# Low halves of weights made early, and lists, taps and fetches moved, in a two-block transformer kernel

## The chip, the cores and the metric

The kernel runs on one core of one Trainium2 chip, in a single launch. The metric is the device time of one execution in microseconds (us); the figure before is the median of three runs. Engine names are those of the profile: PE is the matrix engine, PEld its weight load, DVE the vector engine, ACT the scalar engine, POOL the GpSimd engine, SP the engine that only issues transfers.

## The reference

Two blocks follow each other on one sequence of 512 tokens, 1024 wide, all in float32.

- First block: an RMS norm, one input projection, a sliding-window attention (8 query heads, 2 key heads, blocks of 128) beside a convolution of width 31 over 512 channels with a layer norm and a pointwise product; their concatenation goes through `w_out`, is normed and added. Then a gated feed-forward layer (1024 to 2816 to 1024), normed and added.
- Second block: a norm and one projection; a gated spatial unit; an attention that keeps the 128 best keys of a scored list; two sigmoid gates and an output product. Then `peer`: queries of 8 heads x 2 halves are scored against 128 keys each, the 16 best of each half are combined into 16 experts of 16384 for each head, and the output is the sum over these 128 experts of gate x gelu(x . u_e) x v_e:

```
sub = einsum('bshpd,hpnd->bshpn', q, subkeys)
s_top, i_top = top_k(sub, 16)
best, pos = top_k(s_top[0] + s_top[1], 16)
a = gelu(einsum('td,ted->te', x, u_tab[expert]))
y = einsum('te,ted->td', softmax(best) * a, v_tab[expert])
```

## The kernel before, in words

Tokens lie in four blocks `tb` of 128. A weight comes in units of 128 x 1024 (`unit`, lines 132 to 142): SP's queue loads `raw`, ACT casts it to a rounded high half `whi` (line 138), and DVE subtracts for the low half `wlo` (line 140). Each product is then three matmuls, high x high, high x low and low x high (`mm3`, lines 155 to 158). The rings `raw`, `whi` and `wlo` have four buffers each.

The program is written as one list of calls, and a scheduler orders each engine's instructions from that list; side work (convolution taps, attention, top-k lists) is written as generators, which `advance` draws on beside the projections by a written estimate in us (`CONV_US`, `ATT_US`, `TOPK_US`, `TOP_US`, `R_US`).

- Convolution and first attention (lines 324 to 548). Each channel group has 31 taps; of groups 2 and 3 the first 12 and 8 run on PE as diagonal matmuls (`pe_taps`, line 363), the others on DVE (line 368). `att1(b)` makes scores (435, 439), softmax (446 to 460), transposes (466) and the value product (469). A bias table comes back from DRAM as `rev` (403) and is flipped on PE (405), all four parts ahead of the queries.
- `transition` (248 to 304) ends a layer: sums of squares, `rsqrt` (160 to 165: a DVE instruction, then a power on POOL, line 164), scaling, transposes (183).
- Feed-forward layer (559 to 575): 44 units, 24 matmuls of 512 columns each.
- Second block: index scores (`index_block`), top-k on DVE (`topk`, 709 and 710), queries, then for each `tb` the key and value product into a PSUM bank `kv` (744 to 747), norm and rotation (750 to 758), `turn` (735). The table `wsT` is masked by four POOL instructions (816).
- `peer`. The 16 query units give `sub`; `top_keys` (968 to 977) makes a list for each of 64 (block, half-head) pairs; `keys` (979) combines and builds experts' numbers through one-hots (1030, 1031) and matmuls (1034, 1036); `build` (1091) spreads gates into a table `g_dram`. Beside that PE runs 100 of the 128 blocks of `peer_u` for 320 tokens (`u_block`, 930), the results going to `a_dram`. Tokens past 320 are done by gathered rows (`gathered`, 946): 192 gathers of `peer_u` rows and 128 of `peer_v`, each followed by one DVE instruction (949, 957, 964).
- Last stage (1199 to 1260). For each pair of blocks `second` (1218) multiplies the stored activations `al` by the gates `gl` (line 1228), splits the product into `wvhi` and `wvlo`, and `v_block` runs 18 matmuls of 512 columns for each of 128 blocks of `peer_v`. `al` (line 1211) and `gl` (line 1225) are fetched where they are first used.

```
with order(after[0]):
    lead[0] = S.copy(hi[:, :n], raw[:, :n]).ins
with order(after[1]):
    pace[0] = V.tensor_tensor(lo[:, :n], raw[:, :n], hi[:, :n].bitcast(F32), op=OP.subtract).ins
```

## Time and profile before

| what | value |
|---|---|
| median of three runs | 2129.66 us (2129.12 to 2134.75) |
| the profiled execution | 2132.12 us |
| its span, first to last instruction | 2130.4 us |
| PE busy | 2061.1 us (97%) |
| DVE busy | 1573.1 us (74%) |
| ACT busy | 825.7 us (39%) |
| POOL busy | 520.2 us (24%) |
| mean granted PE clock | 0.988 |
| bytes moved, mean rate | 476.47 MB, 224 GB/s |

A busy PE is one that has a matmul under way; its ends are modelled, so what tells of lost time are the pauses, the engine that ended each, the granted clock, and the number of matmuls in a stretch. Stages with their own limits follow each other: attention and convolution until about 250 us, the feed-forward layer until 590, the second block until 960, `peer`'s queries until 1047, lists and blocks of `peer_u` until 1484, and the products with `peer_v` from there.

### The profile page before, as it was taken

How to read it: one execution, taken by the hardware profiler on the slowest of the kernel's cores; microseconds unless marked ns; L12 is line 12 of the kernel's file. 1: busy time of each engine (PE TensorE's matmuls, PEld its weight loads, DVE VectorE, ACT ScalarE, POOL GpSimd, SP SyncE). 2: the span in 40 equal slices, each digit the busy share in tenths (PEclk: the TensorE clock that was granted, in tenths of full speed). 3: DMA queues.
4: the chain of work that ended last, by engine and by line, in shares of the span. 5: the costliest groups of instructions: out<-in, count | busy, mean ns of one | idle time of the engine just before them, and what ended most of it. 6: DMA issues, size and time to landing. Idle time of an engine off the chain costs nothing.

```text
span 2130.4 us, 29554 instructions
## 1 busy us (share of the span) xinstructions
PE 2061.1 (97%) x11128; PEld 1753.5 (82%) x11128; DVE 1573.1 (74%) x2901; ACT 825.7 (39%) x1339; POOL 520.2 (24%) x383
## 2 busy tenths in 40 slices
PE   7989999999989999999999999999999999999999
PEld 6746888888877877888889899999888878788887
DVE  6974633332268955455699999998999988899997
ACT  5354422221244342333453455555433333333332
POOL 1000000000010000000032222220575656566573
PEclk9998999999999999999999999999999999999999
DMA  5202232333222222333278889899999999999995
GB/s 188 82 28 69 72 107 93 95 99 117 84 87 80 70 89 69 109 124 98 81 288 278 289 299 358 290 365 307 390 394 411 389 402 387 410 402 411 411 399 223
DMA packets 163281, 476.47 MB, mean 224 GB/s; under 512 B 13865, under 2 KB 57265, under 8 KB 161218
## 3 DMA queue, kind: packets, MB, share of 16 engines
q1 hardware_dynamic: 67104, 259.70, 34.2%
q0 software_dynamic: 46656, 169.18, 20.9%
q10 hardware_dynamic: 49378, 45.71, 6.5%
q8 instruction: 87, 1.43, 0.3%
q14 instruction: 56, 0.46, 0.1%
HBM read 432.18 MB, written 42.09 MB: 223 GB/s over the span
## 4 chain that ended last, share of the span: by engine, by line
PE 54%; DVE 21%; issue 13%; DMA 8%; POOL 3%; ACT 2%; DVEq 0%; POOLq 0%; SPq 0%; ACTq 0%
PE bank_a L156 12%; PE bank_a L157 12%; PE bank_a L158 12%; DVE wlo L140 5%; PE bank_b L156 4%; PE bank_b L157 4%; PE bank_b L158 4%; DMA rows<-in_peer_u_dram,gidx 2%; DVE rows L957 2%; POOL rows L941 2%; DMA rows<-in_peer_v_dram,gidx 2%; DMA al<-a_dram 2%; DVE h L964 2%; DVE rows L949 2%; PE bank_b L1108 1%
## 5 line engine op out<-in xcount | busy, mean ns | idle before, releaser
L138 ACT CAST whi<-raw 128x1024 fp32r<-128x1024 f32 (+1 forms) x413 | 431.9, 1047 | 884.0 <-PE bank_a L157 332.0
L140 DVE TENSOR_TENSOR wlo<-raw,whi 128x1024 fp32r<-128x1024 f32 (+1 forms) x413 | 499.9, 1213 | 265.9 <-ACT whi L138 263.6
L156 PE MATMUL bank_a<-xhi,whi 128*128 128x320 f32 (+2 forms) x1600 | 549.3, 344 | 0.8 <-ACT xhi L152 0.8
L158 PE MATMUL bank_a<-xhi,wlo 128*128 128x320 f32 (+2 forms) x1600 | 546.2, 342 | 3.3 <-DVE wlo L140 3.3
L157 PE MATMUL bank_a<-xlo,whi 128*128 128x320 f32 (+2 forms) x1600 | 548.0, 343 | 0.6 <-DVE xlo L153 0.6
L941 POOL DMA_INDIRECT rows<-in_peer_u_dram,gidx x192 | 279.0, 1453 | 553.4 <-DVE gidx L1042 143.1
L158 PEld LDWEIGHTS bank_a<-xhi,wlo 128*128 128x128 f32 x1600 | 303.5, 190 | 31.6 <-DVE wlo L140 5.3
L156 PEld LDWEIGHTS bank_a<-xhi,whi 128*128 128x128 f32 x1600 | 302.8, 190 | 28.3 <-ACT xhi L152 1.8
L157 PEld LDWEIGHTS bank_a<-xlo,whi 128*128 128x128 f32 x1600 | 303.7, 190 | 26.9 <-DVE xlo L153 1.6
L941 POOL DMA_INDIRECT rows<-in_peer_v_dram,gidx x128 | 206.2, 1611 | 115.2 <-DVE h L964 91.2
L164 POOL TENSOR_TENSOR rstd<-rstd,neghalf 128x1 f32<-128x1 f32 (+2 forms) x37 | 25.2, 682 | 844.2 <-DVE rstd L163 832.4
L156 PE MATMUL bank_a<-whi,wvhi 128*128 128x512 f32 x512 | 201.9, 394 | 7.4 <-ACT wvhi L152 7.3
L157 PE MATMUL bank_a<-wlo,wvhi 128*128 128x512 f32 x512 | 202.0, 394 | 1.7 <-DVE wlo L140 1.6
L158 PE MATMUL bank_a<-whi,wvlo 128*128 128x512 f32 x512 | 201.7, 394 | 1.7 <-DVE wvlo L153 1.6
L964 DVE SCALAR_TENSOR_TENSOR h<-rows,ga,h 128x1024 f32<-128x1024 f32 x128 | 164.1, 1282 | 5.6 <-DMA rows<-in_peer_v_dram,gidx 4.2
L957 DVE SCALAR_TENSOR_TENSOR rows<-rows,h 128x1024 f32<-128x1024 f32 x128 | 152.8, 1220 | 9.9 <-DMA rows<-in_peer_u_dram,gidx 9.9
L156 PEld LDWEIGHTS bank_a<-whi,wvhi 128*128 128x128 f32 x512 | 97.0, 189 | 28.7 <-ACT wvhi L152 9.1
L158 PEld LDWEIGHTS bank_a<-whi,wvlo 128*128 128x128 f32 x512 | 97.2, 190 | 24.9 <-DVE wvlo L153 4.2
L157 PEld LDWEIGHTS bank_a<-wlo,wvhi 128*128 128x128 f32 x512 | 97.0, 189 | 21.6 <-DVE wlo L140 2.4
L156 PE MATMUL bank_b<-whi,wvhi 128*128 128x512 f32 x256 | 99.9, 390 | 0.0
L158 PE MATMUL bank_b<-whi,wvlo 128*128 128x512 f32 x256 | 99.6, 389 | 0.0
L157 PE MATMUL bank_b<-wlo,wvhi 128*128 128x512 f32 x256 | 99.6, 389 | 0.0
(403 smaller groups left out, 3272.5 us busy)
## 6 DMA issues: line engine op xcount, KB each, us to landing
raw<-in_wt_dram SPq DMA_DIRECT2D x150, 512.0 KB, 3.6
raw<-in_ut_dram SPq DMA_DIRECT2D x128, 512.0 KB, 5.8
raw<-in_peer_v_dram SPq DMA_DIRECT2D x128, 512.0 KB, 8.0
g_dram<-gt ACTq DMA_DIRECT2D x24, 896.0 KB, 7.9
gl<-g_dram SPq DMA_DIRECT2D x14, 1536.0 KB, 10.6
a_dram<-ab ACTq DMA_DIRECT2D x25, 640.0 KB, 5.6
al<-a_dram SPq DMA_DIRECT2D x25, 640.0 KB, 9.3
rows<-in_peer_u_dram,gidx POOLq DMA_INDIRECT x192, 9.1
```

Of the source, the lines that this page charges most:

```text
L138: lead[0] = S.copy(hi[:, :n], raw[:, :n]).ins
L140: pace[0] = V.tensor_tensor(lo[:, :n], raw[:, :n], hi[:, :n].bitcast(F32), op=OP.subtract).ins
L156: T.matmul(o, lh, rh, start=start, stop=False)
L157: T.matmul(o, lh, rl, start=False, stop=False)
L158: T.matmul(o, ll, rh, start=False, stop=stop)
L164: G.tensor_tensor(r, r, neghalf[:, :shape[1]], op=OP.pow)
L941: G.indirect_dma_start(out=r, out_offset=None, in_=table, in_offset=bass.IndirectOffsetOnAxis(ap=idx[:, k:k + 1], axis=0))
L949: V.scalar_tensor_tensor(r, r, 1.0, hn2, op0=OP.mult, op1=OP.mult, accum_out=ga2[:, k:k + 1])
L957: V.scalar_tensor_tensor(r, r, 1.0, hn3, op0=OP.mult, op1=OP.mult, accum_out=ga[:, k:k + 1])
L964: V.scalar_tensor_tensor(h[3], r, ga[:, k:k + 1], h[3], op0=OP.mult, op1=OP.add)
L1108: T.matmul(gp[:, j, :], o_[:, g2, :, t2], oh1[:, g2, :, t2], start=o_ is ohs[0], stop=o_ is ohs[-1])
```

## The change

Low halves are made ahead: in the feed-forward loop `make_low` runs twice for each of the 22 columns. It loads one of 44 units through POOL's queue, casts it on ACT, subtracts on DVE and stores the low half to DRAM through POOL's queue. The 44 are the 16 units of the queries and the first 28 blocks of `peer_u`. Where a unit has such a low half, `unit` fetches it into `wlo` through ACT's queue in place of the subtraction.

The lists of blocks 0 and 1 are drawn on beside the queries too, behind those of blocks 2 and 3; the written estimates there grow by `LOW_US`. `al` is fetched one step ahead with three buffers, `gl` a group ahead in three pieces. The 12 PE taps of group 2 become 8, and the PE taps are issued inside the attention of blocks 2 and 3 while their DVE taps join at once; the four parts of the bias are spread over the queries; the first products with `w_out` move behind the mean of the layer norm; the four key and value products move beside the query units, evacuated by ACT; the masks of `wsT` are put behind a power; two square sums are added inside the instruction that adds the epsilon.

```diff
-N_PE_TAPS = (0, 0, 12, 8)
+LOW_US = 1.0
+N_PE_TAPS = (0, 0, 8, 8)
-SA_BUFS = 4
+SA_BUFS = 7
+N_EARLY = 28
...
-    def unit(src, n=1024, after=(None, None)):
+    def unit(src, n=1024, after=(None, None), low=None):
...
+        if low is not None:
+            nc.scalar.dma_start(lo[:, :n].bitcast(F32), low[:, :n])
         with order(after[0]):
             lead[0] = S.copy(hi[:, :n], raw[:, :n]).ins
+        if low is not None:
+            return hi, lo
...
+    early = [(wt[p], lows, p) for p in range(wt.shape[0] - 16, wt.shape[0])] + \
+            [(A["ut"][i], ulows, i) for i in [2 * p + j for p in SPAIR for j in range(2)][:N_EARLY]]
+
+    def make_low(wk):
+        if not early:
+            return
+        src, where, key = early.pop(0)
+        raw = wk.tile([128, 1024], F32, name="eraw", bufs=2)
+        nc.gpsimd.dma_start(raw, src)
+        lo = wk.tile([128, 1024], F32R, name="elow", bufs=2)
+        with order(lead[0]):
+            S.copy(lo, raw)
+        with order(pace[0]):
+            V.tensor_tensor(lo, raw, lo.bitcast(F32), op=OP.subtract)
+        where[key] = lowp.tile([128, 1024], F32, name=f"low{len(early)}")
+        nc.gpsimd.dma_start(where[key], lo[:].bitcast(F32))
...
+    def rsqrt2(ssq):
+        r = small.tile([128, 1], F32, name="rstd", tag="rstd1")
+        V.tensor_scalar(r, ssq[:, 0:1], ssq[:, 1:2], EPS, op0=OP.add, op1=OP.add)
+        rooted[0] = G.tensor_tensor(r, r, neghalf[:, 0:1], op=OP.pow).ins
+        return r
...
+            if 1 <= n_ <= 4:
+                band_bias(n_ - 1)
...
             for n_, t in enumerate(zipped(att1(2), att1(3))):
-                if n_ == 3:
-                    us0.extend(next_unit() for _ in range(2))
-                    os0.extend(bank("a") for _ in range(2))
-                    proj_tok(os0, *src1, range(2), 8, 0, us0, 2, 512)
+                if n_ in (4, 6):
+                    c23[n_ // 2 - 2][1]()
                 yield t
...
-        for c in (0, 1):
-            c23[c][1]()
-            da = advance(av, da + ATT_US)
-        c23 = [c_[0] for c_ in c23]
-        cv = chain(cv, zipped(*c23))
+        cv = chain(cv, zipped(*[c_[0] for c_ in c23]))
...
             split(hdhi[:, f, :], hdlo[:, f, :], sg)
+            make_low(wk)
+            make_low(wk)
...
+        kv = bank("b")
+        for k in range(2):
+            mm3(kv[:, :256], cnhi[:, j, k], cnlo[:, j, k], ukv[0][:, k * 256:(k + 1) * 256],
+                ukv[1][:, k * 256:(k + 1) * 256], k == 0, k == 1)
+        S.copy(vv[:, j, :], kv[:, 128:256])
+        S.copy(ksb[:, j, :], kv[:, :128])
...
-    for g in range(4):
-        G.affine_select(out=wsT[:, g, :], in_=wsT[:, g, :], pattern=[[1, 128]], compare_op=OP.is_ge,
-                        fill=0.0, base=0, channel_multiplier=-1)
+    with order(rooted[0]):
+        for g in range(4):
...
-        u = unit(A["ut"][i1])
+        u = unit(A["ut"][i1], low=ulows.get(i1))
...
-            for tb in (0, 1):
-                yield from top_keys(sub[tb], tb, range(16))
+            yield from chain(*todo[1])
...
             while not made2:
-                next(gat)
-            weights2()
-            yield 0.5
+                yield next(gat)
+            yield from weights2()
...
-                    d1 = advance(route, d1 + TOP_US)
+                    d1 = advance(route, d1 + TOP_US + LOW_US)
...
-            todo += [top_keys(sub[tb], tb, range(c4 * 4, c4 * 4 + 4)) for tb in (2, 3)]
+            for tb in (2, 3, 0, 1):
+                todo[tb < 2] += [top_keys(sub[tb], tb, range(c4 * 4 + j, c4 * 4 + j + 2)) for j in (0, 2)]
...
-                d1 = advance(route, d1 + R_US - (g1 if ready else 0.0))
+                more = LOW_US if n4 + j < N_EARLY else 0.0
+                d1 = advance(route, d1 + R_US + more - (g1 if ready else 0.0))
...
+        def load_a(m):
+            if m < len(SPAIR) // 2:
+                state["a", m] = pv.tile([128, 4, N_U], F32, name="al", bufs=3)
+                nc.sync.dma_start(state["a", m], a_dram[m])
+        def load_g(g, k):
...
+                nc.sync.dma_start(state["g", g][:, sl], g_dram[g - N_RES][:, sl])
```

On DVE, between the convolution's input `hc` of group 2 and the scores `sa` of attention blocks 2 and 3 (`acc_311` is group 2, `L364` adds the PE taps, `L368` is a DVE tap), the program before ends so:

```order
L457 TENSOR_TENSOR den<-den,es 128x4
L458 RECIPROCAL den<-den 128x4
L457 TENSOR_TENSOR den<-den,es 128x4
L458 RECIPROCAL den<-den 128x4
L354 SCALAR_TENSOR_TENSOR hc<-sg,bank_a 128x512
L457 TENSOR_TENSOR den<-den,es 128x4
L458 RECIPROCAL den<-den 128x4
L140 TENSOR_TENSOR wlo<-raw,whi 128x1024 x2
L364 TENSOR_TENSOR acc_311<-acc_311,bank_b 128x512
L368 SCALAR_TENSOR_TENSOR acc_311<-hc,cw,acc_311 128x512 x9
```

In the changed program (`acc_313` and `acc_314` are groups 2 and 3, `L402` a DVE tap, `L493` and `L494` the softmax sums) the same place reads:

```order
L402 SCALAR_TENSOR_TENSOR acc_313<-hc,cw,acc_313 128x512 x2
L493 TENSOR_TENSOR den<-den,es 128x4
L402 SCALAR_TENSOR_TENSOR acc_313<-hc,cw,acc_313 128x512
L388 SCALAR_TENSOR_TENSOR hc<-sg,bank_a 128x512
L494 RECIPROCAL den<-den 128x4
L402 SCALAR_TENSOR_TENSOR acc_314<-hc,cw,acc_314 128x512 x3
L493 TENSOR_TENSOR den<-den,es 128x4
L402 SCALAR_TENSOR_TENSOR acc_314<-hc,cw,acc_314 128x512
L494 RECIPROCAL den<-den 128x4
L402 SCALAR_TENSOR_TENSOR acc_314<-hc,cw,acc_314 128x512 x2
```

The taps no longer stand behind the addition of the PE taps, but between the softmax sums that wait for ACT.

On POOL, from the end of the feed-forward layer to the spatial unit, the program before has (`L164` is the power, `L669` the mask of the index scores):

```order
L164 TENSOR_TENSOR rstd<-rstd,neghalf 128x1 x7
L816 AFFINE_SELECT wsT<-wsT 128x128 x4
L164 TENSOR_TENSOR rstd<-rstd,neghalf 128x1 x5
L669 AFFINE_SELECT mask_4374<-mask_4374 128x128
L669 AFFINE_SELECT mask_4375<-mask_4375 128x128
L669 AFFINE_SELECT mask_4376<-mask_4376 128x128
L164 TENSOR_TENSOR rstd<-rstd,neghalf 128x5 x4
```

and the changed one (`L195` and `L202` are powers, `L700` the mask of the index scores):

```order
L700 AFFINE_SELECT mask_4648<-mask_4648 128x128
L700 AFFINE_SELECT mask_4649<-mask_4649 128x128
L700 AFFINE_SELECT mask_4650<-mask_4650 128x128
L195 TENSOR_TENSOR rstd<-rstd,neghalf 128x5 x4
L850 AFFINE_SELECT wsT<-wsT 128x128 x4
L195 TENSOR_TENSOR rstd<-rstd,neghalf 128x1 x4
```

The four masks of `wsT` moved from ahead of a layer end's last power to behind the norms of the queries.

On ACT, at the first blocks of `peer_u`, the changed program reads as follows (`L143` issues the fetch of a low half, `L145` casts a high half, `L971` is the gelu of one block's result, `L1060` belongs to the one-hots); before, `L138` and `L937` alternate there and no fetch stands between them:

```order
L971 ACTIVATE ab<-bank_a 128x320
L143 DMA wlo<-low_2806 128x1024
L971 ACTIVATE ab<-bank_a 128x320
L145 CAST whi<-raw 128x1024
L143 DMA wlo<-low_2813 128x1024
L145 CAST whi<-raw 128x1024
L971 ACTIVATE ab<-bank_a 128x320
L143 DMA wlo<-low_2887 128x1024
L1060 COPY ohh<-sf 128x1024
L145 CAST whi<-raw 128x1024
```

The fetch for block 4 (`low_2806`) is issued behind the gelu of block 0, whose `wlo` buffer it takes.

## Rows read from the trace of the kernel before

**Rows 1.** The page: busy time of each engine.

```profile
PE 2061.1 (97%) x11128; PEld 1753.5 (82%) x11128; DVE 1573.1 (74%) x2901; ACT 825.7 (39%) x1339; POOL 520.2 (24%) x383
```

**Rows 2.** Windows: width, PE PEld DVE ACT POOL busy (count), clock, DMA share, GB/s.

```profile
300.00:480.00 180.00, 180.00 (x796) 149.04 (x795) 61.66 (x67) 52.47 (x66) 0.00 (x0) 1.00 0.31 97
...
650.00:760.00 110.00, 104.66 (x477) 83.78 (x474) 100.71 (x252) 42.89 (x104) 7.87 (x10) 0.97 0.27 88
...
1047.00:1075.00 28.00, 27.74 (x189) 27.36 (x189) 26.60 (x147) 16.30 (x22) 0.00 (x0) 1.00 0.38 123
1075.00:1150.00 75.00, 70.04 (x511) 68.86 (x510) 72.61 (x262) 34.93 (x50) 24.09 (x20) 0.95 0.81 292
1150.00:1480.00 330.00, 321.42 (x2646) 313.10 (x2645) 325.32 (x724) 176.52 (x306) 69.83 (x57) 0.99 0.92 317
1484.00:2126.00 642.00, 631.09 (x2994) 534.19 (x2992) 578.47 (x659) 218.17 (x249) 391.27 (x243) 0.99 0.98 386
```

**Rows 3.** Waits of PE: total us, times, longest.

```profile
PE bank_b L1034 <- DVE ohl L1031: 9.2, 4, 2.5
PE bank_a L156 <- ACT wvhi L152: 7.3, 3, 3.7
...
PE bank_b L466 <- ACT sa L460: 6.4, 2, 4.5
PE bank_b L156 <- DVE qk L757: 4.4, 1, 4.4
...
PE bank_b L405 <- DMA rev<-bdr: 2.7, 2, 1.5
```

**Rows 4.** Window around a pause of PE: the granted clock.

```profile
624.70:628.10 3.40, 3.29 (x14) 2.95 (x15) 2.70 (x7) 1.82 (x5) 1.07 (x2) 0.51 0.00 0
```

**Rows 5.** Timeline of convolution and attention: start us, us, engine, line, instruction, [idle before <-releaser].

```profile
108.52 17.34 PE L363 MATMUL bank_b<-hc,dgs 128*128 128x512 f32 x40
```

**Rows 6.** The same stretch on DVE.

```profile
109.49 0.16 DVE L457 TENSOR_TENSOR den<-den,es 128x4 f32<-128x4 f32 x1 [4.04 <-ACT sa L455]
...
116.43 2.36 DVE L140 TENSOR_TENSOR wlo<-raw,whi 128x1024 fp32r<-128x1024 f32 x2 [3.32 <-ACT whi L138]
...
170.23 0.69 DVE L153 TENSOR_TENSOR catlo<-bank_a,cathi 128x512 fp32r<-128x512 f32 x1 [1.74 <-ACT cathi L152]
171.53 2.48 DVE L518 TENSOR_TENSOR acc<-acc,bank_b 128x512 f32<-128x512 f32 x4 [0.60 <-PE bank_b L513]
```

**Rows 7.** The same stretch on ACT.

```profile
145.58 0.51 ACT L455 ACTIVATE sa<-sa,nm 128x256 f32<-128x256 f32 x1 [9.33 <-DVE nm L449]
```

**Rows 8.** Timeline at the end of the feed-forward layer.

```profile
622.33 1.03 POOL L816 TENSOR_SCALAR_AFFINE_SELECT wsT<-wsT 128x128 f32<-128x128 f32 x4 [4.87 <-DMA wsT<-in_wsT_dram]
...
624.81 1.08 PE L183 MATMUL bank_b<-cst,xs 128*128 128x128 f32 x4 [3.30 <-DVE xs L298]
```

**Rows 9.** Timeline of DVE at the fourth block's query norm.

```profile
705.34 1.13 DVE L755 SCALAR_TENSOR_TENSOR qk<-bank_a,rstd,qkg 128x128 f32<-128x128 f32 x4 [0.76 <-POOL rstd L164]
```

**Rows 10.** Groups by form, DVE, 1047 to 1481 us: count | busy us, mean ns | idle before.

```profile
L140 DVE TENSOR_TENSOR wlo<-raw,whi 128x1024 fp32r<-128x1024 f32 x100 | 121.4, 1214 | 7.7 <-ACT whi L138 7.7
...
L973 DVE FIND_INDEX8 si<-sv,gres 128x8 uint32<-128x128 f32 x32 | 9.2, 287 | 0.0
```

**Rows 11.** Windows: one stretch of the routed stage, columns as in rows 2.

```profile
1112.80:1116.20 3.40, 3.40 (x19) 3.40 (x19) 3.12 (x9) 2.15 (x3) 0.00 (x0) 0.50 1.02 408
```

**Rows 12.** Tile `al`: what its instructions waited for (us, times), and landing times.

```profile
  DMA al<-a_dram: 19.0, 5
  DMA gl<-g_dram: 5.0, 3
...
DMA to landing us min/median/max: 3.9/9.3/15.6
```

**Rows 13.** The page's DMA issues: count, KB each, us to landing.

```profile
raw<-in_ut_dram SPq DMA_DIRECT2D x128, 512.0 KB, 5.8
...
rows<-in_peer_u_dram,gidx POOLq DMA_INDIRECT x192, 9.1
```

More of the change, by code (lines that the diff above doesn't have):

```diff
@@ L158, in mm3 @@
         T.matmul(o, ll, rh, start=False, stop=stop)
+    rooted = [None]
     def rsqrt(ssq, scale, shape, after=None):
@@ L279, in transition @@
                 V.tensor_tensor(xs[:, 512:], os1[tb], g_post[:, 512:], op=OP.mult)
-                s1 = small.tile([128, 1], F32, name="ssq1")
-                V.tensor_tensor(s1, ssq[tb][:, 0:1], ssq[tb][:, 1:2], op=OP.add)
-                r = rsqrt(s1, 1.0 / 1024, [128, 1])
+                r = rsqrt2(ssq[tb])
                 for sl in halves:
@@ L292, in transition @@
             for hf, sl in enumerate(halves):
-                S.activation(xs[:, sl], h[tb][:, sl], AF.Square, accum_out=sq[:, hf:hf + 1])
-            s1 = small.tile([128, 1], F32, name="ssq1")
-            V.tensor_tensor(s1, sq[:, 0:1], sq[:, 1:2], op=OP.add)
-            r = rsqrt(s1, 1.0 / 1024, [128, 1])
+                S.activation(xs[:, sl], h[tb][:, sl], AF.Square, scale=1.0 / 32, accum_out=sq[:, hf:hf + 1])
+            r = rsqrt2(sq)
             for sl in halves:
@@ L400, in tile_layers, with band_bias @@
         flip = cst1[:, 256:384]
-        for j in range(4):
+        def band_bias(j):
             rev = pt_.tile([128, 2, 256], F32, name="rev", bufs=2)
@@ L513, in tile_layers @@
             T.matmul(mu, oneD, acc[c], start=(c == 0), stop=(c == 3))
-        os0.extend(bank("a") for _ in range(2))
-        proj_tok(os0, *src1, (2, 3), 8, 0, us0[:1], 2, 512)
+        src1 = (lambda tb, k: cathi[:, tb, k, :]), (lambda tb, k: catlo[:, tb, k, :])
+        os0 = [bank("a") for _ in range(4)]
+        proj_tok(os0, *src1, range(4), 8, 0, [next_unit()], 2, 512)
         var = bank("b")
@@ L532, in tile_layers @@
         T.matmul(rs, ones, rdg.rearrange("p b t -> p (b t)"), start=True, stop=True)
-        proj_tok(os0, *src1, (2, 3), 8, 2, us0[1:], 2, 512)
+        proj_tok(os0, *src1, range(4), 8, 2, [next_unit()], 2, 512)
         for c in range(4):
@@ L742, in tile_layers @@
     for tb in range(4):
-        kv = bank("b")
-        for k in range(2):
-            mm3(kv[:, :256], cnhi[:, tb, k], cnlo[:, tb, k], ukv[0][:, k * 256:(k + 1) * 256],
-                ukv[1][:, k * 256:(k + 1) * 256], k == 0, k == 1)
-        S.copy(vv[:, tb, :], kv[:, 128:256])
         qk = wk.tile([128, 5, 128], F32, name="qk", bufs=2)
@@ L814, in tile_layers @@
     nc.scalar.dma_start(wsT, A["wsT"])
-    for g in range(4):
-        G.affine_select(out=wsT[:, g, :], in_=wsT[:, g, :], pattern=[[1, 128]], compare_op=OP.is_ge,
-                        fill=0.0, base=0, channel_multiplier=-1)
+    with order(rooted[0]):
+        for g in range(4):
+            G.affine_select(out=wsT[:, g, :], in_=wsT[:, g, :], pattern=[[1, 128]], compare_op=OP.is_ge,
+                            fill=0.0, base=0, channel_multiplier=-1)
     bs = wk.tile([1, 512], F32, name="bs")
@@ L1144, in tile_layers @@
         nc.scalar.dma_start(skT, A["skT"])
-        todo = []
+        todo = [[], []]
         def routed():
-            while todo or not keyed:
-                if todo:
-                    yield from todo.pop(0)
+            while todo[0] or not keyed:
+                if todo[0] or todo[1]:
+                    yield from (todo[0] or todo[1]).pop(0)
                 else:
@@ L1220, in second @@
             i1 = 2 * p
-            if i1 % 8 == 0 and i1 // 8 < N_RES:
-                state["gl"] = gres[i1 // 8]
-            elif i1 % 8 == 0:
-                state["gl"] = pv.tile([128, 24, 8, 16], F32, name="gl", bufs=2)
-                nc.sync.dma_start(state["gl"], g_dram[i1 // 8 - N_RES])
+            if i1 % 8 == 0:
+                state["gl"] = state.pop(("g", i1 // 8))
+            else:
+                load_g(i1 // 8 + 1, i1 % 8 // 2 - 1)
             av = state.pop(p)
@@ L1239, in v_block @@
                         vu[0][:, hf * 512:(hf + 1) * 512], vu[1][:, hf * 512:(hf + 1) * 512], i1 == 0, i1 == 127)
+        load_g(0, 0)
+        load_a(0)
         for j in range(2):
```

35 lines of the change are left out of this document (22 added, 13 removed).

## The prediction

> **What bounds the kernel now.** I read the page's busy line first: PE has a matmul under way for 2061.1 of the span's 2130.4 us, DVE for 74% [rows 1]. So 69 us of pauses on PE and its stretches at half clock are nearly all that an edit off PE can win. Next the windows by stage [rows 2], to see which engine stands closest to the width of its window: in the feed-forward layer PE alone; between 650 and 760 us DVE too (100.71 of 110); in the routed stage (lists, one-hots and blocks of `peer_u`, 1047 to 1480) DVE again (26.60 + 72.61 + 325.32 = 424.5 of 433), with DMA at 0.81 and 0.92; in the last stage DMA at 0.98 and DVE at 578 of 642, under a PE at 631. Then the waits of PE [rows 3] say who ends its pauses: `ohl` and `wvhi` of DVE and ACT, `sa`, `qk`, `rev`. Last the clock: behind a pause of 3.30 us a window of 3.40 us reads 0.51 [rows 4], the lower of the two levels (1.2 of 2.4 GHz), so 1.7 us of matmul time are lost behind a pause of that size, on top of it. I counted twelve such stretches, of which this is one.
>
> The sum is made against the profiled execution, 2132.12 us: its span of 2130.4 and 1.7 around it. It stands 2.5 above the median of 2129.66.
>
> **The change part by part.**
>
> *Convolution and attention, 108 to 187 us.* Before, PE runs 20 taps in 17.34 us [rows 5], 12 of them group 2's, so DVE, whose taps stand behind the addition of those, cannot start before 108.5 + 10.4 = 118.9; it idles 4.04 and 3.32 before it, and 1.74 and 0.60 at the end of the stretch [rows 6]. ACT waits 9.33 us for the row maxima of blocks 2 and 3 [rows 7], whose scores PE makes only behind the taps, and PE then waits 6.4 for `sa` [rows 3]. Afterwards DVE taps fill the places between the softmax sums, as the order shows, the scores come ahead of the taps, PE has four taps less (17.34 x 4/20 = 3.5 us) and DVE four more (a 128x512 two-input instruction takes 2.48/4 = 0.62 [rows 6], so 2.5). On DVE: 4.04 + 3.32 + 1.74 + 0.60 = 9.7 of idle time goes, `rev` gives 2.7 [rows 3], the taps 3.5 - 2.5 = 1.0: 13.4. On PE: 6.4 + 2.7 + 3.5 and two half clocks of 1.7, 16.0. What is late next is DVE itself, which then runs without idle time to the mean of the layer norm. I take **-12**, below both, bounds -17 and -5 (only `rev`, and PE's taps less DVE's, with one half clock).
>
> *Masks of `wsT`.* The four masks wait 4.87 us on POOL for their transfer, and the power of the last token block stands behind them; PE waits 3.30 for it [rows 8]. Now the power is ahead. Some 0.2 of the pause stays, so 3.1 and the half clock of 1.7: **-4.8**, bounds -5 and -3. Behind the masks POOL has then nothing that PE needs before the `sub` products.
>
> *Two square sums added in one instruction.* One small DVE instruction (0.16 us, as the smallest of [rows 6]) less on each of the chains that end three transitions, two of them in a row: **-1**, bounds -1.5 and 0.
>
> *Keys and values.* The pause of 4.4 on `qk` [rows 3] goes from its place. But DVE is busy 100.71 of 110 us [rows 2] and the fourth `qk` starts at 705.3 behind a pause of 0.76 for a power [rows 9]; PE needs it for the turn whatever stands ahead. Only the pauses for powers are filled: **-2**, bounds -4.4 and +2 (16 more products fall beside the queries, and ACT evacuates them).
>
> *Feed-forward layer.* 44 casts and 44 subtractions. DVE works 61.66 and ACT 52.47 of 180 us there, DMA moves 97 GB/s [rows 2]. A subtraction is 1.214 us [rows 10], in all 53; an ACT instruction averages 52.47/66 = 0.80, in all 35. The 22 columns end by about 480, so DVE comes to some 57%, and 88 transfers of 0.524 MB in 230 us add 200 GB/s, to about 300, under the 408 of [rows 11]. **0**, bounds 0 and +8: PE is at its spacing (180/796 = 0.226 us) with no pause, and 8 would be forty pauses of 0.2, one for almost every unit. In the queries 16 fetches replace 16 subtractions: hidden, 0. The lists drawn there use DVE that has half its time free.
>
> *Routed stage.* DVE loses 28 subtractions of 1.214 = 34 us, and 21 lists of five instructions near 0.287 [rows 10], about 30, now done beside the queries; it gets 6 gathers more at about 1.2, 7 us (counted from the order: 79 for 73). So 424.5 becomes 367. PE has 27.74 + 70.04 + 321.42 = 419.2 busy, less what the clock of 0.95 and 0.99 takes (3.8 + 3.3): 412. PE becomes the bound, and the ceiling is 433 - 412 = 21 us. Against it stands DMA. From 1075 to 1150 it moves 292 x 75 = 21.9 MB [rows 2]; at 3.5 us for a block (24 matmuls of 28/189 = 0.148) 21 blocks fit at most, so I count 19 low halves on top, 9.9 MB; 31.8 MB at 408 GB/s [rows 11] take 78 us, 3 more than the stretch. So I give this stretch +2 and take from the rest its pauses and clock, 330 - 321.42 + 3.3 = 12: together **-10**, bounds -21 and +15 (the fetches late, rival 1). The rate of 408 is the highest of the trace and held for 3.4 us; the mean of the last stage, 386 over 642 us [rows 2], would make 82 us of it, +7.
>
> The Trainium skill ("DMA: Bandwidth & Descriptors", section "Bandwidth") puts what one core can draw from its memory near 358 GB/s; by it the stretch of 31.8 MB would take 89 us, and the sum would end at -26 instead of -38. The trace speaks against it: 386 over the whole last stage and 408 in windows [rows 2, 11].
>
> *Last stage.* `al` makes what needs it wait 19.0 us in 5 pieces, `gl` 5.0 in 3; the landing is 9.3, at most 15.6 [rows 12], while DVE has 578 of 642 busy. Fetched a step ahead, both are there. PE's pauses for `wvhi` are 7.3 [rows 3], and two of them bring half clocks, 3.4: 10.7 at most. No bytes change and DMA stays at 0.98, so part of the lateness stays with the blocks of `peer_v`: **-8**, bounds -11 and 0.
>
> Sum: -12 - 4.8 - 1 - 2 + 0 - 10 - 8 = **-37.8**. Against the profiled execution 2132.1 - 37.8 = 2094.3; against the median 2129.7 - 37.8 = **2092**.
>
> **The rivals.**
>
> 1. *Low halves late.* The fetch of block n waits, on ACT's queue, for the gelu of block n - 4, whose buffer it takes (the order shows it). A buffer's round is landing L, the block (3.5) and about 1.5 for gelu and issue; four buffers give a period of (L + 5.0)/4. Above L = 9 this exceeds 3.5. For it: a gather of rows lands in 9.1 and `al` in up to 15.6 [rows 12, 13]; DMA is near full there. Against: the same 512 KB of `raw` land in 5.8 [rows 13]. At L = 11.5 the period is 4.1, 28 blocks lose some 18 us, and the stage gives +8 for -10: 2110. Chance 0.13.
>
> 2. *The pauses only move.* DVE's order in attention, or one-hots on DVE in the routed stage, end PE's pauses as now: half of the -12 and of the -12 remain, and 6 of the -8: 2110. For it: each one-hot chain goes over ACT, POOL and DVE in turn, and PE waits 9.2 for only four of them [rows 3]. Against: DVE has 57 us more room. Chance 0.12.
>
> 3. *PE runs free.* The routed stage wins the whole 21 and attention 16: 2077; with the last stage's 11, 2074. For it: DVE was the bound at 98%. Against: DMA at 0.92 behind 1150. Chance 0.10.
>
> 4. *Slower.* The mechanism of rival 1 at a higher price: with the 28 fetches landing in L = 17, as `al` nearly did, the period is 5.5 and the blocks lose 28 x 2.0 = 55, all else kept: 2147. From L = 15.5 on (28 x 1.6 = 45 against 38) the change is no gain. For it: every other transfer of the stage shares the same 16 DMA engines. Against: the landing of 5.8 would have to triple. Chance 0.08.
>
> [...] In this trace raw loads on SP's queue and gathers on POOL's land in 5.8 and 9.1 beside each other; none on ACT's is there to compare.
>
> That the change does not do what it says I exclude: the order has the 28 fetches, and the stores end near 480, some 480 us before the first is read.
>
> **How the numbers follow.** The forecast, 2092, has 0.57 and by its terms' bounds (not all at one end) a range of its own of 2076 to 2108. Rivals 1 to 3 add 0.35 and 4 adds 0.08. The range 2065 to 2120 leaves out 4, the far end of 1 and a little of 3 below, about 0.15. A measurement of this kernel tells 0.3%, 6.4 us, from no change: 2123 to 2136. Of rivals 1 and 2 about 0.05 reaches there, of 4 about 0.01. Faster: 0.57 + 0.35 - 0.05 = 0.87; same 0.06; slower 0.07.
>
> **What would show it.** Right: no `rev` and no `sa` of 4.5 among PE's waits; ACT's idle 9.33 gone and the layer norm's mean near 159 instead of 171.5; the four masks behind the power on POOL and no PE pause of 3.3 near 624; fewer than half of the twelve half-clock stretches; `wvhi` off PE's list; DVE near 367 between the last query and the last stage, PE over 98% there; low halves landing in under 9 us. Wrong: PE waiting for `wlo` by DMA in the first 28 blocks (1 or 4); `ohl` as long as before (2); pauses of PE in the feed-forward layer; the last stage as long as before, its pauses at `raw` instead.

## The result, and the profile after

| what | before | changed |
|---|---|---|
| median of four runs | 2129.39 us | 2165.78 us (2161.18 to 2169.49) |
| ratio to before, 95% interval | 1 | 1.0163 (1.0141 to 1.0185) |
| span of the profiled execution | 2130.4 us | 2164.9 us |
| mean granted PE clock | 0.988 | 0.981 |
| bytes moved, mean rate | 476.47 MB, 224 GB/s | 545.70 MB, 252 GB/s |

The change made the kernel 36 us slower; a gain of 38 was forecast. The page's busy line of the changed kernel answers to [rows 1]:

```profile
PE 2072.9 (96%) x11120; PEld 1756.7 (81%) x11120; DVE 1574.5 (73%) x2885; ACT 865.8 (40%) x1383; POOL 573.2 (26%) x471
```

PE has 8 matmuls less and is busy 12 us longer (its clock is lower, and the ends are modelled), and its pauses grew from 69 to 92 us. DVE's busy time is what it was: the 44 subtractions were moved, not saved.

To see where the time went, the span is cut at four instructions that both kernels have. Views of the tiles `g_post`, `g_next` and `wvhi` of the kernel before (operation, count, shortest/median/longest ns, first and last start):

```profile
L94 ACTq DMA_DIRECT2D g_post<-in_gvec_dram x2: 334/336/339, 190.3 to 485.6; - x2
L94 ACTq DMA_DIRECT2D g_next<-in_gvec_dram x3: 358/455/617, 190.6 to 891.5; - x3
L156 PE MATMUL bank_a<-whi,wvhi x512: 388/389/632, 1498.9 to 2124.3; 128*128 128x512 f32 x171
```

and of the changed kernel:

```profile
L98 ACTq DMA_DIRECT2D g_post<-in_gvec_dram x2: 334/337/340, 183.4 to 485.9; - x2
L98 ACTq DMA_DIRECT2D g_next<-in_gvec_dram x3: 357/456/497, 183.8 to 887.7; - x3
L185 PE MATMUL bank_a<-whi,wvhi x512: 387/389/632, 1513.2 to 2158.8; 128*128 128x512 f32 x171
```

The two fetches of `g_post` mark the ends of attention and of the feed-forward layer, the last of `g_next` the end of the second block ahead of `peer`, and the first matmul with `wvhi` the beginning of the last stage, which I count to the end of the last matmul (2126.5 and 2161.1). The table has these five stretches for both kernels and for all runs below, each from its one profiled execution. The medians in its last column are those of four to ten executions; those of one kernel lie 5 to 12 us apart. The kernel before was measured again beside each group of runs, with medians of 2129.9 to 2131.5.

| kernel | attention | feed-forward | second block | queries and routed stage | last stage | median us |
|---|---|---|---|---|---|---|
| before | 190.3 | 295.3 | 405.9 | 607.4 | 627.6 | 2129.4 |
| changed | 183.4 | 302.5 | 401.8 | 625.5 | 647.8 | 2165.8 |
| e1 al, gl as before | 179.5 | 304.7 | 402.2 | 631.3 | 632.9 | 2153.7 |
| e2 no lows of peer_u | 184.8 | 303.9 | 401.7 | 609.5 | 644.1 | 2146.6 |
| e3 both | 183.3 | 304.3 | 402.2 | 607.6 | 631.6 | 2131.8 |
| e4 no lows, al, gl as before | 179.6 | 294.3 | 401.5 | 603.9 | 633.7 | 2117.3 |
| e5 lows of an eighth | 183.8 | 302.7 | 401.7 | 609.6 | 648.8 | 2149.3 |
| e6 lows fetched by SP | 184.0 | 305.9 | 401.8 | 615.1 | 644.6 | 2155.2 |
| e7 no lows, al and gl ahead | 179.4 | 294.8 | 401.8 | 607.5 | 645.0 | 2135.6 |
| e8 the same, issued by POOL | 180.0 | 294.5 | 401.7 | 605.2 | 658.6 | 2147.6 |
| e9 three eraw | 180.1 | 295.4 | 401.4 | 626.5 | 645.3 | 2156.3 |
| e10 no lows, al ahead | 184.5 | 294.1 | 401.5 | 605.6 | 624.9 | 2109.2 |
| e11 no lows, gl ahead | 183.9 | 295.0 | 402.0 | 606.2 | 651.4 | 2144.3 |
| e15 gl whole, 5 gather buffers | 179.6 | 294.3 | 401.5 | 607.4 | 654.0 | 2149.4 |
| e18 e4 with 5 gather buffers | 180.3 | 294.6 | 401.7 | 607.5 | 654.6 | 2150.8 |
| e20 gl ahead in two pieces | 183.2 | 294.0 | 401.4 | 605.6 | 646.3 | 2140.9 |
| e19 lows mended | 183.2 | 295.1 | 402.2 | 615.7 | 623.7 | 2120.8 |

So the change won 6.9 in attention and 4.1 in the second block, and lost 7.2 in the feed-forward layer, 18.1 in queries and routed stage, and 20.2 in the last stage: +34.5, the difference of the spans. Windows of the changed kernel, columns as in [rows 2]:

```profile
300.00:480.00 180.00, 175.18 (x763) 143.69 (x762) 100.20 (x102) 85.13 (x102) 34.93 (x66) 0.99 0.87 299
650.00:760.00 110.00, 103.20 (x470) 81.76 (x469) 97.00 (x239) 43.01 (x105) 8.57 (x13) 0.95 0.29 86
1075.00:1150.00 75.00, 61.62 (x405) 58.61 (x402) 62.28 (x312) 30.52 (x44) 23.32 (x23) 0.91 1.01 394
1150.00:1480.00 330.00, 319.36 (x2659) 310.35 (x2658) 283.89 (x427) 174.81 (x307) 78.15 (x59) 0.99 0.95 328
1514.00:2160.00 646.00, 620.21 (x2875) 520.31 (x2874) 558.66 (x633) 210.95 (x238) 383.62 (x234) 0.98 0.95 370
```

Against [rows 2] two things stand out. From 1075 to 1150 DMA is full (1.01) and PE issues 405 matmuls where it issued 511 (523 in the window 3.8 us later, by which the second block ended later before). And DVE is far below its window from 1150 to 1480, 283.89 of 330 where it was 325.32, and yet PE's busy time is not above what it was (319.36 and 321.42). Waits of PE over the whole span (us in total, times, longest), which answer to [rows 3]:

```profile
PE bank_a L186 <- DVE wlo L149: 15.6, 5, 6.6
PE bank_a L187 <- DMA wlo<-low: 11.3, 7, 3.7
...
PE bank_a L185 <- ACT wvhi L181: 8.1, 6, 2.0
PE bank_b L773 <- DVE qk L660: 6.8, 2, 4.7
...
PE bank_a L185 <- ACT whi L145: 4.4, 5, 2.0
...
PE bank_b L221 <- DVE xs L332: 2.7, 5, 0.8
PE bank_b L1068 <- DVE ohl L1065: 2.4, 1, 2.4
...
PE bank_a L185 <- ACT sg L600: 1.9, 1, 1.9
```

`rev`, `sa` of 4.5, `xs` of 3.3 and most of `ohl` are gone. In their place stand `wlo` by DVE (last stage), `wlo` by DMA (routed stage), and `whi` and `sg` by ACT (one pause of 2.0 and one of 1.9 in the feed-forward layer; the rest of `whi` is in the routed stage). `qk` stays, at another place and somewhat longer (6.8 for 4.4).

### The profile page after: what moved, and what is told of

Same layout as the page of the kernel before. It is cut to its first block, busy times and chain, and to the rows that moved or that the text cites. A ratio compares the mean times of both kernels' runs of the same rounds, so it can differ in the third digit from the quotient of the medians.

```text
span 2164.9 us, 29888 instructions
## 1 busy us (share of the span) xinstructions
PE 2072.9 (96%) x11120; PEld 1756.7 (81%) x11120; DVE 1574.5 (73%) x2885; ACT 865.8 (40%) x1383; POOL 573.2 (26%) x471
## 2 busy tenths in 40 slices
DMA packets 186323, 545.70 MB, mean 252 GB/s; under 512 B 16425, under 2 KB 59825, under 8 KB 186050
## 4 chain that ended last, share of the span: by engine, by line
PE 17%; issue 13%; DVE 10%; DMA 8%; POOL 2%; ACT 0%; SPq 0%; DVEq 0%; POOLq 0%; ACTq 0%
DMA gl<-g_dram 5%; DVE h L998 4%; PE bank_a L187 4%; PE bank_a L185 4%; PE bank_a L186 4%; POOL rows L975 2%; DVE wlo L149 2%; DMA raw<-in_peer_v_dram 2%; PE bank_b L185 2%; PE bank_b L186 2%; PE bank_b L187 2%; DMA rows<-in_peer_u_dram,gidx 1%; PE bank_b L1145 1%; DVE wvlo L182 1%; DVE gl L1280 1%
## 5 line engine op out<-in xcount | busy, mean ns | idle before, releaser
L145 ACT CAST whi<-raw 128x1024 fp32r<-128x1024 f32 (+1 forms) x413 | 430.7, 1045 | 695.1 <-PE bank_a L186 177.7
L149 DVE TENSOR_TENSOR wlo<-raw,whi 128x1024 fp32r<-128x1024 f32 (+2 forms) x369 | 446.9, 1213 | 189.3 <-ACT whi L145 188.8
L185 PEld LDWEIGHTS bank_a<-xhi,whi 128*128 128x128 f32 x1600 | 304.7, 191 | 37.7 <-ACT whi L145 5.6
L176 DVE TENSOR_TENSOR elow<-eraw,elow 128x1024 fp32r<-128x1024 f32 x44 | 53.8, 1224 | 103.9 <-ACT elow L174 103.7
L202 POOL TENSOR_TENSOR rstd<-rstd,neghalf 128x1 f32<-128x1 f32 x20 | 13.0, 652 | 386.7 <-DVE rstd L201 383.2
```

What stands on the lines that cost most here:

```text
L176: V.tensor_tensor(lo, raw, lo.bitcast(F32), op=OP.subtract)
L185: T.matmul(o, lh, rh, start=start, stop=False)
```

## The experiments

**e1, e2, e3: the two large losses apart.** e1 puts the fetches of `al` and `gl` back where they are first used, e2 takes the 28 low halves of `peer_u` away, e3 does both.

```diff
-N_EARLY = 28
+N_EARLY = 0
```

> The changed kernel with al and gl fetched where they are first used, as before; all else stays. First theory (the prefetches take places on SP's queue in which they wait for a buffer that DVE has still to release, 51.8 us in 17 waits, and the raw blocks behind them come late): the last stage, 648 us in the changed kernel's trace against 628 before, falls back to about 628, and the time to about 2146. Rival (the last stage is longer because of what the routed stage leaves it, not because of the fetches): it stays near 648 and the time near 2165.

> The changed kernel without the 28 low halves of peer_u blocks (the 16 of the queries stay); DVE subtracts for all blocks of peer_u. First theory (the fetched low halves fill the DMA engines between 1075 and 1150, 409 GB/s, and PE waits for them): the stretch from the last query to the last stage loses the 18 us it had grown by, and the time is about 2148. Rival (the lists and gathers that moved make that stretch longer): DVE gets its 34 us of subtractions back on top, and the time is 2165 or above.

> Both of the edits before together. If the two losses are independent, about 2129, level with the kernel before (the 7 us that attention won and the 7 that the feed-forward layer lost cancel). If the late prefetches follow from the late low halves, as one backlog, it is no better than the better of the two, about 2146.

Measured: 2153.7, ratio 1.0109 (1.0083 to 1.0135); 2146.6, 1.0075 (1.0058 to 1.0092); 2131.8, 1.0007 (0.9997 to 1.0017). The places are as the first theory says: e1 takes 14.9 off the last stage and nothing off the others but attention, e2 takes 16.0 off queries and routed stage and 3.7 off the last. The losses add: 12.1 + 19.2 = 31.3 for 34.0 of both. e1 came out 8 us above its number, since the last stage stays 5 above that of before and the routed stage read 631.3. What e1 does not show is why the fetch ahead is late; its first theory named SP, and e8 and e10 speak against that.

**e4: no low halves at all.** The list `early` is left empty; `al` and `gl` as before.

> No low halves made early at all, and the old fetches: attention, masks, sums, keys and values and lists as changed. First theory (casts of ACT wait for eraw, 119 us in 39 waits, and twice the cast that PE needs stands behind one): the two pauses of 2 us near 306 and 326 and their half clock go, 5 to 7 us, and the time is about 2122. Rival (the subtractions for the query units, now beside the lists, cost as much): 2129.

Measured: 2117.3, ratio 0.9944 (0.9925 to 0.9963), now faster than before. The feed-forward layer falls from 304.3 (e3) to 294.3, three us more than expected, and the queries' stretch by 3.7. What made the pauses is seen in the changed kernel: waits of ACT between 240 and 490 us,

```profile
ACT elow L174 <- DMA eraw<-in_ut_dram: 74.5, 25, 7.0
ACT elow L174 <- DMA eraw<-in_wt_dram: 44.4, 14, 4.5
```

and the timeline of ACT at the first pause (start us, us, line, instruction, idle before it and releaser):

```profile
307.00 1.04 ACT L174 CAST elow<-eraw 128x1024 fp32r<-128x1024 f32 x1 [4.00 <-DMA eraw<-in_wt_dram]
307.95 1.04 ACT L145 CAST whi<-raw 128x1024 fp32r<-128x1024 f32 x1
```

beside that of PE:

```profile
309.04 0.50 PE L185 MATMUL bank_a<-xhi,whi 128*128 128x512 f32 x1 [1.98 <-ACT whi L145]
```

ACT stood 4 us at a cast that nobody needed soon, the cast that PE needed stood behind it, and PE paused 1.98. A second such pause, 1.90 at 326 for `sg`, which ACT writes behind such a cast, was followed by a stretch near half clock:

```profile
329.00:332.40 3.40, 3.18 (x9) 2.30 (x8) 3.23 (x4) 2.02 (x3) 0.69 (x2) 0.55 0.72 245
```

ACT was busy 85 of 180 us there: its share of busy time does not tell that its queue stands still.

**e5 and e6: why the low halves come late in the routed stage.** e5 fetches an eighth of each low half of `peer_u` and uses it for all eight parts, so that it leaves out seven eighths of the low halves; e6 issues the fetches from SP, and its edit is shown.

```diff
-            nc.scalar.dma_start(lo[:, :n].bitcast(F32), low[:, :n])
+            nc.sync.dma_start(lo[:, :n].bitcast(F32), low[:, :n])
```

> The changed kernel, the low halves of the 28 peer_u blocks fetched by an eighth (128 of 1024 columns, 64 KB for 512), at the same place of ACT's queue; the matmuls use these columns for all eight parts, so seven eighths of the low halves are left out. If the bytes are the cause (DMA full from 1100 to 1150), the pauses of PE for wlo by DMA go, the last stage begins near 1485 instead of 1513, and the time is about 2137. If the cause is that the fetch is issued late, behind the gelu of four blocks earlier on ACT's queue, the pauses stay at half their size or more and the time is 2155 or above.

> The changed kernel with all 44 fetches of low halves issued by SP, each right behind its raw block, instead of by ACT. If the bytes are the cause, no change: 2159 to 2172. If the place behind the gelu is, the fetch starts up to a block earlier and the time is about 2150.

Measured: 2149.3, ratio 1.0080 (1.0055 to 1.0105), and 2155.2, 1.0114 (1.0090 to 1.0138). e5 takes 15.9 off the stretch, e6 10.4. So the bytes are the larger part of the cause, and the place behind the gelu a part of it too; neither theory of the pair holds alone. e5's total stands 12 above its number, since it gave the stretch 10 us beyond what it had lost, for DVE's freed time, and these did not come. Two windows from 1100 to 1150, first of the changed kernel:

```profile
1100.00:1150.00 50.00, 40.55 (x254) 39.19 (x252) 41.93 (x220) 19.85 (x28) 11.35 (x11) 0.86 1.02 410
```

then of e5:

```profile
1100.00:1150.00 50.00, 45.84 (x323) 45.12 (x323) 46.01 (x233) 25.77 (x34) 10.52 (x10) 0.93 0.94 347
```

With most of the bytes gone PE issues 323 matmuls for 254, and the clock loses 0.07 of 50 us, 3.5, instead of 7. How late a low half was, the changed kernel's timeline shows, on ACT:

```profile
1125.36 0.44 ACT L971 ACTIVATE ab<-bank_a 128x320 f32<-128x320 f32 x1 [2.14 <-PE bank_a L187]
1126.19 0.45 ACTq L143 DMA_DIRECT2D wlo<-low  x1
```

and on PE:

```profile
1139.89 0.63 PE L187 MATMUL bank_a<-xhi,wlo 128*128 128x320 f32 x1 [3.71 <-DMA wlo<-low]
```

The fetch is issued behind the gelu of one block, at 1126.2, and the block four later waits for it until 1139.9: 13.7 us. In e5's waits of PE from 940 to 1500 `wlo` by DMA is down to 1.9 in 2, but these stand ahead of it:

```profile
PE bank_b L1069 <- DVE ohl L1066: 8.4, 4, 3.4
PE bank_a L187 <- DVE wlo L149: 7.0, 4, 3.7
```

The one-hots end PE's pauses as before (9.2 in 4 [rows 3]), and the ring of low halves by DVE adds some. e5, with 28 subtractions less on DVE and an eighth of the bytes for them, takes 609.6 us for the stretch; e2, where DVE makes them all, 609.5. The 34 us that DVE was to save are worth nothing here.

**e7, e8, e10, e11: why the fetch ahead is a loss in the last stage.** All have no low halves. e7 has `al` and `gl` ahead, e8 the same from POOL's queue, e10 only `al`, e11 only `gl`.

```diff
-                nc.sync.dma_start(state["a", m], a_dram[m])
+                nc.gpsimd.dma_start(state["a", m], a_dram[m])
...
-                nc.sync.dma_start(state["g", g][:, sl], g_dram[g - N_RES][:, sl])
+                nc.gpsimd.dma_start(state["g", g][:, sl], g_dram[g - N_RES][:, sl])
```

> No low halves at all, but al and gl fetched ahead as in the change (the run without low halves and with the old fetches gave 2117). If the prefetch is a loss by itself, 2129 to 2137 (12 us by the pair with low halves, 15 by the pair without those of peer_u, up to 20 by the last stage of the trace). If it loses only because late low halves leave the last stage less slack, 2117 or below.

> As the run before, with the fetches of al and gl issued by POOL instead of SP. If the loss comes from SP standing at these fetches (they wait for a buffer of DVE, raw blocks queue behind), it goes: 2117 or down to 2109, the 8 us that the prediction gave the prefetch. If it comes from more bytes at once on the DMA engines, it stays: as the run before.

> No low halves, al fetched a step ahead with three buffers as in the change, gl as before (both as before gave 2117, both ahead 2136). If gl's three pieces are the loss (the first is let go by the same release of its buffer as the whole was, the last stands some 4 us later behind a raw block on SP), al alone is free of it: 2117 or up to 8 us below, since al's waits of 26 us on DVE go. If al is the loss (it stands at its buffer on SP's queue), about 2130 or above.

> No low halves, gl fetched in three pieces as in the change, al as before. If the pieces are the loss: about 2133. If al is: about 2117.

Measured: e7 2135.6, ratio 1.0026 (1.0011 to 1.0040), 18 above e4, so the fetch ahead is a loss by itself. e8 2147.6, 1.0088 (1.0063 to 1.0113): worse. In e8 raw blocks no longer queue behind `al` and `gl` (ACT waits for `raw` of `peer_v` 11.2 us, in e7 121.8), and the last stage is still 13.6 longer. By itself e8 proves little, since POOL now stands at these fetches, 64.9 us in 11 waits, ahead of its gathers. e10 settles it: 2109.2, 0.9893 (0.9877 to 0.9910). There the raw blocks come as late as in e7, first e7, then e10:

```profile
ACT whi L145 <- DMA raw<-in_peer_v_dram: 121.8, 42, 9.4
ACT whi L145 <- DMA raw<-in_peer_v_dram: 115.6, 38, 9.3
```

and yet its last stage is the second shortest of the table. Late raw blocks are not the cause, and that part of e1's first theory falls. SP's long stand at the buffers of `al` goes with the split `gl`: 52.4 us in 17 in e7, where DVE is late at the products that free them, 24.4 in 17 in e10 and 23.0 in 17 before. e11 2144.3, 1.0069 (1.0050 to 1.0087). `al` ahead gains 8.1 on e4 by the medians (10.9 by the ratios; executions of one kernel lie 8 to 12 us apart); its wait goes from 26.2 in 6 to 1.9 in 1, and PE's for `wvhi` from 10.4 in 5 to 5.7 in 4. `gl` ahead in three pieces loses 27.0.

Waits of DVE in the changed kernel's last stage, against 19.0 in 5 for `al` and 5.0 in 3 for `gl` in [rows 12]:

```profile
DVE gl L1280 <- DMA gl<-g_dram: 46.8, 8, 11.3
```

`al` waits no more, `gl` nine times as long. One group's fetch shows why. Timeline of SP in e10, where `gl` is fetched whole at its first use:

```profile
1974.84 0.33 SPq L1278 DMA_DIRECT2D gl<-g_dram  x1
```

and of DVE there, at the product that needs it:

```profile
1986.75 1.56 DVE L1281 TENSOR_TENSOR gl<-al,gl 128x640 f32<-128x640 f32 x2 [4.21 <-DMA gl<-g_dram]
```

The same group in e11, SP:

```profile
1998.60 0.80 SPq L1256 DMA_DIRECT2D gl<-g_dram  x2
2000.93 1.47 SPq L139 DMA_DIRECT2D raw<-in_peer_v_dram  x2
2002.45 0.43 SPq L1256 DMA_DIRECT2D gl<-g_dram  x1
```

and DVE:

```profile
2016.46 0.83 DVE L1281 TENSOR_TENSOR gl<-al,gl 128x640 f32<-128x640 f32 x1 [10.15 <-DMA gl<-g_dram]
```

The three pieces that the code asks for one pair apart leave SP nearly together: there are two `gl` buffers, and the first piece waits until DVE has released the one of two groups before, as the whole transfer did. The instruction that releases it, first in e10, then in e11:

```profile
1973.87 0.95 DVE L182 TENSOR_TENSOR wvlo<-gl,wvhi 128x768 fp32r<-128x768 f32 x1
1997.62 0.95 DVE L182 TENSOR_TENSOR wvlo<-gl,wvhi 128x768 fp32r<-128x768 f32 x1
```

In both it ends 0.02 to 0.03 us before SP issues the transfer. So nothing comes earlier. The last piece stands behind two raw blocks, 3.85 us after the first, and lands 14.0 us after its issue; the whole 1.5 MB of e10 landed in 11.9. The product of a group needs all pieces, so DVE waits 10.15 instead of 4.21, its queue of subtractions and gathered rows stands behind the product, and PE pauses 4.7 at the next `wlo`. A whole transfer asked for ahead with two buffers was not run, so what the split costs beside the place of its last piece stays open.

**e20: two pieces.**

```diff
-            else:
+            elif i1 % 8 < 6:
                 load_g(i1 // 8 + 1, i1 % 8 // 2 - 1)
...
-                sl = slice(8 * k, 8 * k + 8)
+                sl = slice(12 * k, 12 * k + 12)
```

> No low halves, al as before, gl ahead in two pieces of 768 KB instead of three of 512 KB. In SP's order the two stand side by side in 5 of 14 groups, in the others one to three raw blocks stand between them, as they stand ahead of the last piece of three. If the place of the last piece is the loss, it is near that of three pieces, 2135 to 2145; if the small size of the pieces is, about half of it, 2128.

Measured: 2140.9, ratio 1.0047 (1.0030 to 1.0064), near three pieces, as the place of the last piece would have it. It is not decisive, since number and place of the pieces changed together: in nine of its 14 groups the second piece still stands behind raw blocks; its waits for `gl` fall to 25.9 in 5 and those for `al` come to 29.0 in 6.

**e15 and e18: gl really ahead.** A third buffer for `gl` costs two of the seven gather buffers; e18 takes these two from e4 and changes nothing else.

```diff
-GBUFS = 7
+GBUFS = 5
...
-                    state["g", g] = pv.tile([128, 24, 8, 16], F32, name="gl", bufs=2)
+                    state["g", g] = pv.tile([128, 24, 8, 16], F32, name="gl", bufs=3)
```

> No low halves, al as before; gl in one transfer, issued a group ahead into one of three buffers (two gather buffers less, 5 for 7, make the room). The theory that gl's fetch is bound by the release of its buffer says that its waits on DVE (10.8 us in 2 without low halves and with the old fetches, 51 in 9 with both ahead) go to nearly nothing and the time is 2117 or up to 5 us below; a gain is small, since PE waits little there. Rival (DMA is full in the last stage and any transfer that comes sooner makes another one late): raw blocks come later and it is 2120 or above.

> No low halves, al and gl as before, and 5 gather buffers instead of 7: the control of the run with gl ahead in three buffers (2149). If the missing gather buffers made that loss, about 2145 here; gl ahead in whole then cost nothing, or gained 0 to 5. If gl's early transfer made it, 2117 to 2122 here.

Measured: e15 2149.4, ratio 1.0095 (1.0078 to 1.0112); e18 2150.8, 1.0096 (1.0076 to 1.0116). The wait for `gl` does fall, from 10.8 in 2 in e4 to 4.6 in 2, as the release of the buffer would have it, but the time rose by 32, and by itself this run looked like a proof against a fetch ahead. The control has the same time: the gather buffers make the loss, and `gl` ahead gains nothing that these runs can tell. Waits in e18's last stage:

```profile
DVE rows L991 <- DMA rows<-in_peer_u_dram,gidx: 32.3, 29, 3.2
...
PE bank_a L185 <- ACT wvhi L181: 25.2, 8, 6.5
```

In e4 these read 5.1 in 6 and 10.4 in 5. With five buffers the gathered rows are late, and DVE, which takes its instructions in order, passes that on.

**e9: the feed-forward layer.** `eraw` gets three buffers, all else as changed.

```diff
-        raw = wk.tile([128, 1024], F32, name="eraw", bufs=2)
+        raw = wk.tile([128, 1024], F32, name="eraw", bufs=3)
```

> The changed kernel with three buffers for eraw instead of two, so that the loads of the early units run one unit further ahead of ACT's cast. If ACT standing at these casts (119 us in 39 waits) makes PE's pauses at 306 and 326, the feed-forward layer loses them, 302.5 us in the changed kernel's trace falls to about 295, and the time to about 2158. If the load is late because POOL issues it only behind the store that waits for DVE, the buffer changes little: 2162 to 2168.

Measured: 2156.3, ratio 1.0125 (1.0108 to 1.0142). The layer takes 295.4 us, as before the change (295.3), and PE's waits from 250 to 590 us come to 1.1 us (4.8 in the changed kernel). Waits of ACT between 240 and 490 us:

```profile
ACT elow L174 <- DMA low<-elow: 50.8, 20, 7.5
...
ACT elow L174 <- DMA eraw<-in_wt_dram: 4.1, 1, 4.1
```

The 119 us at `eraw` are gone but for 4.1. ACT still stands 50.8 at the stores that free `elow`, without harm to PE: it is not every stand that costs, but one with a cast behind it that PE needs.

**e19: the low halves mended.** `gl` as before, the low halves fetched by SP, three `eraw`.

> The changed kernel with the three mends that the runs point to: gl as before (al stays ahead), the low halves fetched by SP behind their raw blocks, three buffers for eraw. If the losses add up, 2165.8 less 27 (gl), 10.6 (SP) and 9.5 (eraw): about 2119, and the low halves still cost the 10 us by which this stands above the run without them and with al ahead (2109). If the bytes of the 28 low halves are what the fetch by SP can't mend, 2125 or above. Below 2109 the low halves would pay.

Measured: 2120.8, ratio 0.9953 (0.9936 to 0.9969), where 2119 was expected if the three losses add up. They do, and what stays is 11.6 above e10, which has no low halves: 10.1 of it in queries and routed stage. Its window there:

```profile
1075.00:1150.00 75.00, 62.76 (x430) 61.22 (x429) 59.82 (x268) 35.98 (x47) 21.62 (x20) 0.91 1.03 409
```

DMA is full for all 75 us, and PE issues 430 matmuls where e10, whose second block ends within 0.4 us of e19's, issues 483 at a DMA share of 0.87. Raw blocks that are issued there land in 10.5 us and gathered rows in 13.4 (medians; before 5.3 and 7.6). So the low halves still cost 10 us when they are issued elsewhere; that it is their bytes is read from this window and from e5; no run takes the bytes alone out of e19. The fastest of all is e10, 1.1% faster than before and 2.6% than the change.

## Why the prediction was wrong

**The second block** (-7.8 forecast, -4.1 measured). The masks of `wsT` were right: the 3.3 at `xs` is gone, the longest now 0.8, and the clock from 624.7 to 628.1 reads 1.00. The mis-sized term is keys and values, -2, where the stated danger came: "PE needs it for the turn whatever stands ahead", and PE waits 6.8 for `qk` where it waited 4.4.

**Attention** (-12 forecast, -6.9 measured, in other executions of the same code up to -10.9). The steps came as described: taps fill DVE, `rev` and `sa` are gone, and the mean of the layer norm starts at 166.0 instead of 171.5 (near 159 was forecast). Mis-sized were the pauses that stayed and the clock (the executions at -10.9 have nearly the 12):

```profile
158.49 0.69 DVE L182 TENSOR_TENSOR catlo<-bank_a,cathi 128x512 fp32r<-128x512 f32 x1 [1.74 <-ACT cathi L181]
...
166.04 2.47 DVE L547 TENSOR_TENSOR acc<-acc,bank_b 128x512 f32<-128x512 f32 x4
```

DVE still stands 1.67 and 1.74 for `cathi` with five taps behind it, where the sum had counted such idle time as gone, and the last section has the clock.

**The feed-forward layer** (0 forecast, bounds 0 and +8; +7.2). The failed step is the 0, by which "PE is at its spacing (180/796 = 0.226 us) with no pause" was to stay so; it was argued from shares of busy time: DVE 57%, DMA 300 GB/s, both nearly as forecast (100.20 of 180 and 299). The room was there, but ACT's queue runs in order and stood at `eraw`; e9 gives the 7 us back. Of the new wait on ACT it was not asked what is queued behind it.

**The routed stage** (-10 forecast, +18.1 measured with the queries). Two steps failed. First the price of the bytes, "3 more than the stretch". The rate was right (410 GB/s, share 1.02). By the Trainium skill's figure near 358 ("DMA: Bandwidth & Descriptors", section "Bandwidth") the sum would still have had the wrong sign; the section gives the figure for both cores of a memory domain streaming. This kernel runs on one core, which held 394 over 75 us in the changed kernel and 409 in e19; the figure is not a bound here. But a stretch that was full did not cost only what exceeded it: a transfer in it landed later (the low half above took 13.7 us, where 9 was the limit, and e19's raw blocks 10.5 for 5.3), PE waited 10.5 us in 6 for low halves by DMA between 940 and 1500, and half clocks took 7 of 50 us. Rival 1 had this mechanism and its price of 18; e6 shows its part behind the gelu, 10 us, e5 the bytes, 16, of which the two share some. Second, "PE becomes the bound, and the ceiling is 433 - 412 = 21 us": DVE's load did fall as forecast (373.3 us from 1047 to 1480, 367 forecast), but e5, with 34 us less on DVE and an eighth of the bytes, is no shorter in the stretch than e2. PE's pauses were chains through `ohl` and `wlo`, each a wait for one instruction, and not a lack of DVE time over the stage. That is rival 2. Without any low half the lists moved beside the queries bring the stretch to between 603.9 and 607.5 in eight kernels, 607.4 before: 3.5 us at most.

On the queue the Trainium skill ("DMA: Bandwidth & Descriptors", section "Issuing engines are not separate DMA queues") says that transfers of SP, ACT and GpSimd run on the same engines and interleave. The runs agree: from 1100 to 1150 us it is 410 GB/s in e19 with the fetch on SP and 410 in the changed kernel with it on ACT. What the issuing engine can move is when a transfer starts, by what stands ahead of it in that engine's order, and to this I put e6's 10 us.

**The last stage** (-8 forecast, +20.2 measured). The step that failed is "Fetched a step ahead, both are there". For `al`, which got a third buffer, it held, and e10 gains 8.1; that this is so near the -8, which was meant for both fetches, is luck. For `gl`, which kept two, a call placed earlier in the program moves no transfer, since the release of the buffer sets it, and the split put its last piece behind raw blocks. SP's order is fixed in the program like the orders that were read of ACT, DVE and POOL, so it could have been read beforehand; the prediction took SP as told by the code. That the split `gl` makes the loss is shown by e10 and e11. Argued from timelines, and not shown by a run of its own, is the place of the last piece against the number and size of the pieces.

**The sum.** Rival 4 had the sign right, at 2147, by one mechanism with 55 us at its end. The measured 2166 came of three: rival 1's at about its price, the feed-forward layer near its upper bound of +8, and `gl`, for which the text had no price above 0. Together with the gains of the routed and the last stage that did not come (-10 and -8) they make 63.5 of the 72.3 us between the sum of -37.8 and the measured +34.5.

**Readings that were wrong in themselves.** 408 GB/s is not the highest rate of the trace before: three of the page's 40 slices, 53 us each and all in the last stage, read 411. There are transfers on ACT's queue to compare: the stores `a_dram`, 640 KB, land there in 5.6. Rival 2's sum, with 6 of the -8 remaining, gives 2106 and not 2110. None of these turns the sum.

## What to carry to other kernels

A fetch is ahead only if its buffer is: read from the issuing engine's order and the release of the buffer when it can start, before the code that asks for it earlier is given a gain. Whether work that is moved beside idle engines is hidden shows in the order of their queues, not in their shares of busy time: for each new wait name the next instruction behind it that PE needs. And on a stage whose DMA was near full (0.81 to 0.92), trading 1.2 us of DVE for 0.5 MB of traffic was a loss, even though DVE looked like the bound.
